# A PEER expert layer: four one-hot buffers, placing that begins with one group, and the list steps moved behind the first activation split

## Chip, cores and metric

One core of one Trainium2 chip runs the whole program. Its engines are named as in the profile: PE (matrix multiply; PEld is its weight load), DVE (vector), ACT (activation), POOL (GpSimd, which also issues the indirect transfers), SP (issues the plain transfers). The metric is the device time of one execution in microseconds; lower is better. The time before is the median of three runs, 1680.32 us (1677.39 to 1680.75).

## What is computed

A two-layer encoder trunk on x of 256 tokens by 1024 features, fp32. Layer 0 mixes tokens by multi-head latent attention, layer 1 by sparse attention. After each comes the part that matters here, a PEER mixer: every token picks 16 of 16,384 experts in each of 8 heads (128 picks per token), and the output is the weighted sum of the picked experts' rows:

```python
def per_block(args):                    # x_blk: 128 tokens, e_blk/g_blk: their picks and gates
    u = w_down[e_blk]
    a = jnp.einsum('td,ted->te', x_blk, u).astype(jnp.float32)
    hg = (jax.nn.gelu(a, approximate=False) * g_blk).astype(w_up.dtype)
    return jnp.einsum('te,ted->td', hg, w_up[e_blk]).astype(x_blk.dtype)
```

Each sublayer ends in x <- LayerNorm(alpha * x + sublayer(x)).

## The kernel before

**Numbers.** Every fp32 operand is split into two fp16 parts, `hi` (a cast on ACT, L166) and `lo` (the rest, on DVE, L175); a product is three matmuls (hi by hi, hi by lo, lo by hi). DVE also sums the remainders, which a check at the end uses.

**Weights.** The 128 x 1024 weight blocks come as one stream (`Stream`): `raw` (6 buffers) from HBM, then `hi` and `lo` (6 buffers each). `ws.get()` hands out a block, splits three blocks ahead and loads five more ahead of that. SP issues the loads of blocks at fixed places (L220); POOL issues those of listed blocks by indirect transfers with addresses from the table `up_at` (L218).

**PEER, down stage (d).** The kernel does not gather picks token by token. It multiplies all tokens with all 128 blocks of `down` (128 experts each), in 64 steps of two blocks (loop at L1511, `b0` = 0, 2, ..., 126). One step is 48 matmuls of 128 x 256. Meanwhile DVE chooses the experts (`choose`). Once they are chosen, the gates are **placed** into the matrix A (experts by tokens), four tokens to a group, 64 groups: `prepare` (L1357) builds a one-hot `hot` (L1361) and `gate` (L1363 on DVE, L1367 on ACT) for a group in buffers with the tags V and U, and `place` (L1370) multiplies them into G, 12 matmuls with those for `seen`, which counts the experts in use. A group is prepared in one step and placed behind the matmuls of the next. With `END = 8` the groups are spread so that the last is placed at `b0 = 120`. Where gates are placed already, a step's gelu is multiplied in by DVE (L1525).

**Lists.** When all groups are placed, `lists` (L1390) finds with DVE which experts any token uses. It is a generator with 23 stops: the loop takes three steps of it per `b0` (`list_on(3)`), the up stage one per block until block 11 (`HEAD - 9`), and then all that is left. Its results are the tables `up_at` and `act_at`. Rows of A go to DRAM by `store` (L1493, SP).

**Up stage (y).** The first `DENSE = 46` blocks of `up` are multiplied whole; of the others only listed rows, 72 blocks of 128 rows each. The first `HEAD = 20` dense blocks come in front, the other 26 stand among the listed ones (`_up_order`, L77). A dense block or one listed for both halves of the tokens is 12 matmuls of 128 x 512, one listed for one half is 6. For listed rows, `gather` (L1580) fetches the activations from DRAM by POOL into tiles with the tags V and U, three groups ahead. `cut(n)` (L1596) splits a pair of activations: `xh` on ACT, `xl` on DVE, four pairs deep. `cut(0)` stands at the start of the up stage. Stores go on until block 17, the first three groups are gathered at block 16. The stage ends in `finish` with the layer norm.

**Order.** A scheduler orders the instructions of each engine, except where the program writes the order out: what goes through `dve(...)` is kept in program order on DVE from the moment `chains["dve"]` is set (all groups placed) until the lists are done, and so is `pe(...)` on PE. In that stretch a list step, the lo split of a block, a product (L1525) and the lo half of a cut stand on DVE exactly as written. [...]

**Buffers.** The pool `ohp` has two buffers per tag, V and U, 2 KB per partition each. The one-hots, the lists' scratch and the gathered activations all use them, one after the other.

Of the kernel before, what the change touches and what calls it, by code (L numbers as in the profile page):

```python
# [15 lines left out]
AF = mybir.ActivationFunctionType  # L16
ALU = mybir.AluOpType
AX = mybir.AxisListType

P = 128  # L20
T = 256
D = 1024
NC = D // P
# [42 lines left out]
LEAST, MOST, ROW, SMALL = 64.0, 2.0 ** 40, 4.0, 2.0 ** -24  # L66
BOTH, MOSTLY = 128, 704
CHECKS = 7 * P
DENSE, HEAD = 46, 20
JB, JO, TB, ROWTAIL = 24, 16, 16, 32  # L70
BOTHS = JB + TB
LISTED = BOTHS + 2 * JO
END = 8
CHUNKED = 4


# [251 lines left out]
def tile_trunk(ctx: ExitStack, tc: tile.TileContext, ins, out: bass.AP, short, shared):  # L328
# [3 lines left out]
    def pool(name, bufs, **kw):  # L332
        return ctx.enter_context(tc.tile_pool(name=name, bufs=bufs, **kw))
# [5 lines left out]
    const = pool("const", 1)  # L339
    dram = pool("dram", 1, space=bass.MemoryType.DRAM)  # L340
    small = pool("small", 3)
    ohp = pool("ohp", 2)
    psp = pool("psp", 4, space=bass.MemoryType.PSUM)
    pyp, arena, mhalf, sound = shared["pyp"], shared["arena"], shared["mhalf"], shared["sound"]

# [3 lines left out]
    def ps(name):  # L349
        return psp.tile([P, 512], F32, tag="ps", name=name)  # L350
# [94 lines left out]
    def dve(emit):  # L445
        return link("dve", emit)
# [16 lines left out]
    def proj(o, blk, w=P, late=False):  # L463

        h, l = blk
        if late:
            for c in range(NC):
                mm(o, h[:, c * w : (c + 1) * w], xh[:, c, :], c == 0, False)
                mm(o, h[:, c * w : (c + 1) * w], xl[:, c, :], False, False)
            for c in range(NC):  # L470
                ins = mm(o, l[:, c * w : (c + 1) * w], xh[:, c, :], False, c == NC - 1)
            return ins
        for c in range(NC):
            s = slice(c * w, (c + 1) * w)
            ins = mm3(o, (h[:, s], l[:, s]), (xh[:, c, :], xl[:, c, :]), c == 0, c == NC - 1)
        return ins
# [690 lines left out]
    def peer(li):  # L1167
# [337 lines left out]
        def list_on(n):  # L1505
            for _ in range(n):
                next(listing[0], None)

        groups = prepared = 0
        ready = False  # L1510
        for b0 in range(0, NKEYS, 2):  # L1511
            p = ps(f"d{b0}")
            pv = p.rearrange("p (j t) -> p j t", t=T)
            chosen = ready
            for j in range(2):
                proj(pv[:, j, :], ws.get())
                ready = ready or spend(PACE)
            if b0 == 0:
                chains["pe"] = None
            t0 = 4 * groups  # L1520
            if t0 < T:
                nc.scalar.activation(A[:, b0 : b0 + 2, t0:], pv[:, :, t0:], AF.Gelu, scale=1.0 / unit)
            if t0 > 0:
                nc.scalar.activation(pv[:, :, :t0], pv[:, :, :t0], AF.Gelu, scale=1.0 / unit)
                dve(lambda: nc.vector.tensor_tensor(A[:, b0 : b0 + 2, :t0], A[:, b0 : b0 + 2, :t0], pv[:, :, :t0],  # L1525
                                                    op=ALU.mult))
            while groups < prepared:
                place(groups, b0 + 2)
                groups += 1
            if chosen:  # L1530
                left = max(1, (NKEYS - (END if short else 4) - b0) // 2)
                want = min(64 - groups, -(-(64 - groups) // left))
                assert want <= 3, b0
                for _ in range(want):
                    prepare(prepared, nc.gpsimd if want == 1 else nc.vector)
                    prepared += 1
            if short:
                if groups >= 32:
                    store(0, b0)
                    store(0, b0)  # L1540
                if groups == 64:
                    if listing[0] is None:
                        chains["dve"] = None
                        listing[0] = lists()
                    list_on(3)
                    store(1, b0)
                    store(1, b0)
        assert groups == 64, groups
        if not short:
            chains.pop("pe")  # L1550

        lnar = Arena(arena)
        y4 = [[py(2 * t + n, f"y{t}{n}") for n in range(2)] for t in range(2)]
        parts = {}

        def operand(k):
            if k % 2 == 0 and k not in parts:
                a = A[:, k : k + 2, :]
                slot = slice(k % NC, k % NC + 2)
                hh, al = xh[:, slot, :], xl[:, slot, :]  # L1560
                total = split.total("most")
                split.high(hh, a, A_UNIT)
                split.low(al, a, A_UNIT, hh, total)
                for j in range(2):
                    parts[k + j] = (hh[:, j, :], al[:, j, :])
            return parts[k]

        held = []

        def middle_loads():  # L1570
            held.append(load_x(lnar, keep))
            held.append(load_affine(lnar, li, 1))
            if last and short:
                least()
                split.seen = BOTH + split.n["most"]
                weigh_up(0, 0, split.seen)

        gathered, made = {}, {}

        def gather(g):  # L1580
# [15 lines left out]
        def cut(n):  # L1596
# [11 lines left out]
            dve(lambda: split.low(al, a, A_UNIT, hh, total))  # L1608
            made[n] = [(hh[:, j, :], al[:, j, :]) for j in range(2)]

        if short:
            cut(0)
            for i, (n, slot, tiles) in enumerate(USES):
                if i == FIRSTS[n]:
                    cut(n + 1)
                    if PAIRS[n][0] == "listed":
                        gather(PAIRS[n][1] + 3)
                if i < len(USES) - STAGGER:
                    rows(y4, made[n][slot], ws.get(), i == 0, False, tiles)
                if i < HEAD - 9:  # L1620
                    list_on(1)
                if i == HEAD - 9:
                    list_on(99)
                    chains.pop("dve")
                    chains.pop("pe")
                if i < HEAD - 3:
                    store(0, NKEYS)
                    store(1, NKEYS)
                if i == HEAD - 4:
                    assert stored == [NKEYS, NKEYS], stored  # L1630
                    for g in range(3):
                        gather(g)
                if i == len(USES) // 2:
                    middle_loads()
            items = [(made[n][slot], tiles) for n, slot, tiles in USES[-STAGGER:]]
        else:
            for k in range(NKEYS - STAGGER):
                rows(y4, operand(k), ws.get(), k == 0, False)
                if k == 64:
                    middle_loads()  # L1640
            items = [(operand(k), (0, 1)) for k in range(NKEYS - STAGGER, NKEYS)]
# [18 lines left out]
    def first(o):  # L1660

        queue = queue_of()
        idle = ps("idle")
        some = iotac.rearrange("p c k -> p (c k)")

        def busy(n, w=P):
            for _ in range(n):
                queue("pe", lambda: nc.tensor.matmul(idle[:, :w], iota16, some[:, :w], start=True, stop=True))

        def x_high(c, engine="act"):  # L1670
            queue(engine, lambda: split.high(xh[:, piece[c], :], xt[:, piece[c], :], X_UNIT, engine))

        def x_low(c):
            total = split.total("both")
            return queue("dve", lambda: split.low(xl[:, piece[c], :], xt[:, piece[c], :], X_UNIT, xh[:, piece[c], :],
                                                  total))

        def w_low(i):
            s = slice(512 * i, 512 * i + 512)
            total = split.total("both")  # L1680
            queue("dve", lambda: split.low(lo0[:, s], raw0[:, s], W_UNIT, hi0[:, s], total))

        def passes(w, x, *pieces):
            for c in pieces:
                for k in (2 * c, 2 * c + 1):
                    queue("pe", lambda: mm(o, w[:, k * P : (k + 1) * P], x[:, k, :], k == 0 and w is hi0 and x is xh,
                                           k == NC - 1 and x is xl))

        for i in range(2):
            s = slice(512 * i, 512 * i + 512)  # L1690
            queue("act", lambda: split.high(hi0[:, s], raw0[:, s], W_UNIT))
        w_low(0)
        w_low(1)
        for c in range(4):
            x_high(c)
            last = x_low(c)
        busy(WARM, 512)
        for c in range(2):
            passes(hi0, xh, c)
            passes(lo0, xh, c)  # L1700
        passes(hi0, xl, 0, 1)
        busy(2)
        for c in range(2, 4):
            passes(hi0, xh, c)
            passes(lo0, xh, c)
        passes(hi0, xl, 2, 3)
        return last
# [98 lines left out]
```

## Time and profile before

| what | us |
|---|---|
| median of the runs | 1680.32 |
| profiled execution | 1676.38 |
| its span | 1674.6 |
| PE busy in it | 1606.8 |
| layer 0: d stage, placing, up stage begin near | 142, 304, 533 |
| layer 1: d stage, placing, up stage begin near | 988, 1148, 1377 |
| listed rows of layers 0 and 1 begin on POOL near | 573, 1418 |

The profile comes from one execution. A row of a timeline has the start in us, the length in us, the engine, the line of the program, the operation, "out<-in" by the names of tiles, and a count; in brackets stands the idle time before it and what ended that. A row of waits reads "engine tile line <- what it waited for: us in total, times, longest". The windows give each engine's busy time in a stretch and PE's granted clock as a share of full speed.

### The profile page before, as it was taken

The numbers are of one execution on the slowest core, as the hardware profiler recorded it, in microseconds if no ns is written. First come the engines' busy times: TensorE is split into PE (matmuls) and PEld (weight loads), VectorE is DVE, ScalarE is ACT, GpSimd is POOL, SyncE is SP. The second block draws the span as 40 slices with busy tenths as digits, with TensorE's granted clock in tenths as the row PEclk, the third lists the DMA queues.
The fourth block names the chain that finished last, engine by engine and source line by source line (L and its number), as shares of the span: only waits on it lengthen the run. The fifth ranks groups of instructions, "written<-read, shape, count | busy, mean of one in ns | idle before, by whom it ended". The sixth has DMA issues, their size and how long they took to land.

```text
span 1674.6 us, 33334 instructions
## 1 busy us (share of the span) xinstructions
PE 1606.8 (96%) x12449; PEld 1164.4 (70%) x12449; DVE 1349.2 (81%) x3212; ACT 1064.7 (64%) x1863; POOL 527.6 (32%) x419
## 2 busy tenths in 40 slices
PE   9999999899998999999999999998999989999995
PEld 7678888799996444444577688887999974444442
DVE  8689999788998757676788799998889988566665
ACT  7666647688885446555578666565888764445553
POOL 2011255000000278877032012441000000788772
PEclk9999999999999999999999999999999999999998
DMA  9445656545757878888855555555447568678783
GB/s 348 158 166 174 199 180 210 172 162 172 240 176 235 284 232 279 268 279 269 287 192 180 169 192 181 188 196 194 152 157 246 184 205 292 228 260 267 258 281 121
DMA packets 139964, 361.44 MB, mean 216 GB/s; under 512 B 13713, under 2 KB 56849, under 8 KB 139793
## 3 DMA queue, kind: packets, MB, share of 16 engines
q1 hardware_dynamic: 112880, 268.51, 47.8%
q0 software_dynamic: 26624, 90.20, 16.5%
q8 instruction: 99, 1.62, 0.4%
q14 instruction: 73, 0.59, 0.1%
q10 hardware_dynamic: 288, 0.52, 0.1%
HBM read 333.35 MB, written 25.82 MB: 214 GB/s over the span
## 4 chain that ended last, share of the span: by engine, by line
PE 51%; issue 13%; DVE 11%; DMA 11%; POOL 10%; ACT 3%; SPq 0%; POOLq 0%; DVEq 0%; ACTq 0%
PE d L452 34%; DMA raw<-in_up,up_at 6%; PE y L452 5%; POOL raw L218 5%; DVE lo L175 5%; PE G L452 3%; PE pq L452 2%; PE seen L452 2%; ACT hi L166 2%; POOL V L1593 1%; POOL U L1587 1%; POOL V L1587 1%; DMA U<-abuf,act_at 1%; POOL U L1593 1%; PE qw L452 1%
## 5 line engine op out<-in xcount | busy, mean ns | idle before, releaser
L175 DVE SCALAR_TENSOR_TENSOR lo<-raw,hi 128x1024 f16<-128x1024 f32 (+2 forms) x550 | 696.8, 1277 | 207.5 <-ACT hi L166 203.4
L166 ACT ACTIVATE hi<-raw 128x1024 f16<-128x1024 f32 (+2 forms) x550 | 570.0, 1049 | 374.9 <-DMA raw<-in_up,up_at 166.9
L452 PE MATMUL d<-xh,lo 128*128 128x256 f16 x2048 | 559.3, 273 | 1.6 <-DVE lo L175 1.6
L452 PE MATMUL d<-xh,hi 128*128 128x256 f16 x2048 | 559.5, 273 | 0.0
L452 PE MATMUL d<-xl,hi 128*128 128x256 f16 x2048 | 559.3, 273 | 0.0
L452 PEld LDWEIGHTS <-hi 128*128 128x128 f16 x5016 | 489.3, 98 | 59.0 <-issue 1.5
L218 POOL DMA_INDIRECT raw<-in_up,up_at x144 | 182.5, 1268 | 612.1 <-DMA raw<-in_up 561.8
L452 PEld LDWEIGHTS <-xh 128*128 128x128 f16 x1904 | 185.4, 98 | 232.0 <-issue 12.9
L452 PE MATMUL y<-hi,xl 128*128 128x512 f16 x880 | 265.4, 381 | 11.1 <-DVE xl L175 11.1
L452 PE MATMUL y<-hi,xh 128*128 128x512 f16 x880 | 265.6, 381 | 5.2 <-ACT hi L166 2.8
L452 PE MATMUL y<-lo,xh 128*128 128x512 f16 x880 | 265.8, 381 | 3.6 <-DVE lo L175 3.6
L452 PEld LDWEIGHTS <-lo 128*128 128x128 f16 x2508 | 245.9, 98 | 33.1 <-DVE lo L175 3.6
L1367 ACT ACTIVATE gate<-hot,rest 128x128 f16<-128x128 f16 x512 | 167.3, 406 | 22.3 <-DVE hot L1361 20.7
L452 PEld LDWEIGHTS <-xl 128*128 128x128 f16 x952 | 93.0, 98 | 125.2 <-DVE xl L175 13.8
L255 POOL TENSOR_TENSOR lo<-raw,hi 128x1024 f16<-128x1024 f32 x27 | 62.0, 2295 | 213.6 <-ACT hi L253 182.1
L452 PE MATMUL G<-gate,hot 128*128 128x128 f16 x1024 | 98.2, 221 | 15.7 <-DVE gate L1363 15.7
L1361 DVE TENSOR_TENSOR hot<-iota,place 128x1024 f16<-128x1024 f16 x128 | 87.9, 688 | 26.5 <-PE G L452 25.7
L452 PEld LDWEIGHTS <-hot 128*128 128x128 f16 x1536 | 93.8, 114 | 17.6 <-DVE gate L1363 7.0
L452 PE MATMUL seen<-gate,hot 128*128 128x128 f16 x512 | 90.3, 220 | 0.0
L1282 POOL TENSOR_TENSOR arena<-arena 128x800 f32<-128x800 f16 x32 | 70.4, 2200 | 63.0 <-DVE arena L1279 63.0
L251 ACT ACTIVATE raw<-raw 128x1024 f32<-128x1024 f32 x27 | 28.5, 1056 | 93.1 <-DMA raw<-in_down 82.1
L1363 DVE TENSOR_TENSOR gate<-hot,gate 128x512 f16<-128x512 f16 x128 | 87.3, 682 | 0.0
(269 smaller groups left out, 1807.2 us busy)
## 6 DMA issues: line engine op xcount, KB each, us to landing
raw<-in_down SPq DMA_DIRECT2D x256, 512.0 KB, 3.4
raw<-in_up SPq DMA_DIRECT2D x92, 512.0 KB, 6.1
abuf<-arena SPq DMA_DIRECT2D x80, 256.0 KB, 4.1
raw<-in_peer_q SPq DMA_DIRECT2D x24, 512.0 KB, 4.4
raw<-in_dsa_qk SPq DMA_DIRECT2D x16, 512.0 KB, 4.3
raw<-in_mla_w_o SPq DMA_DIRECT2D x8, 512.0 KB, 5.2
arena<-in_peer_q SPq DMA_DIRECT2D x8, 512.0 KB, 5.3
raw<-in_dsa_v SPq DMA_DIRECT2D x8, 512.0 KB, 5.9
```

What stands on the lines that cost most here:

```text
L166: return nc.scalar.copy(o, src) if unit == 1.0 else nc.scalar.mul(o, src, unit)
L175: return nc.vector.scalar_tensor_tensor(o, src, unit, hi, op0=ALU.mult, op1=ALU.subtract, accum_out=total)
L218: self.nc.gpsimd.indirect_dma_start(t, None, table, bass.IndirectOffsetOnAxis(ap=at, axis=0))
L251: self.act(lambda: nc.scalar.mul(raw, raw, unit))
L255: nc.gpsimd.tensor_tensor(lo, raw, hi if short else hi.bitcast(F32), op=ALU.subtract)
L452: return pe(lambda: nc.tensor.matmul(o, l, r, start=start, stop=stop, skip_group_check=True))
L1282: nc.gpsimd.tensor_tensor(o.rearrange("p k c -> p c k"), same, cell[t][:, h, :, None].to_broadcast([P, CELLS, TOPK]), op=ALU.mult)
L1361: nc.vector.tensor_tensor(hot, iota4[:, None].to_broadcast([P, 2, P, 4]), place16[:, :, None, four].to_broadcast([P, 2, P, 4]), op=ALU.is_ ...
L1363: engine.tensor_tensor(gate[:, 0], hot[:, 1].rearrange("p c j -> p j c"), gate16[:, four, None].to_broadcast([P, 4, P]), op=ALU.mult)
L1367: nc.scalar.mul(gate[:, 1, j, :], hot[:, 1, :, j], rest[:, t : t + 1])
L1587: nc.gpsimd.indirect_dma_start(t[:, 2 * slot : 2 * slot + 2, :].rearrange("p a b -> p (a b)"), None, abuf, bass.IndirectOffsetOnAxis(ap=at ...
L1593: nc.gpsimd.indirect_dma_start(t[:, 2 + h, :], None, halves, bass.IndirectOffsetOnAxis(ap=at, axis=0))
```

## The change

Six edits. [...] `END` goes from 8 to 6, and a step may prepare at most one group more than are placed already, so that the steps place 1, 2, 3 and then two groups each, the last at `b0 = 122`. `cut(0)` moves from the start of the up stage into the last d step, behind its matmuls and ahead of its products. The last d step takes no list steps any more. `HEAD` goes from 20 to 24: block 15 is where the lists must be done, 20 where the first gathers are issued, and 22 dense blocks stay among the listed ones. In the first projection of layer 0, `busy` issues four small filler matmuls rather than two, with another tile as the moving operand. The functions `gather` and `cut` are moved up unchanged so that the loop can call them.

```diff
-DENSE, HEAD = 46, 20
+DENSE, HEAD = 46, 24
-END = 8
+END = 6
...
-    ohp = pool("ohp", 2)
+    ohp = pool("ohp", 4 if short else 2)
...
             if b0 == 0:
                 chains["pe"] = None
+            if short and b0 == NKEYS - 2:
+                cut(0)
             t0 = 4 * groups
...
-                for _ in range(want):
+                for _ in range(min(want, 1 + groups)):
                     prepare(prepared, nc.gpsimd if want == 1 else nc.vector)
                     prepared += 1
...
-                    list_on(3)
+                    if b0 < NKEYS - 2:
+                        list_on(3)
...
         if short:
-            cut(0)
             for i, (n, slot, tiles) in enumerate(USES):
...
         def busy(n, w=P):
+            moving = some[:, :w] if w > P else iota4[:, :, 0]
             for _ in range(n):
-                queue("pe", lambda: nc.tensor.matmul(idle[:, :w], iota16, some[:, :w], start=True, stop=True))
+                queue("pe", lambda: nc.tensor.matmul(idle[:, :w], iota16, moving, start=True, stop=True))
...
-        busy(2)
+        busy(4)
...
-    nc = bacc.Bacc("TRN2", target_bir_lowering=False, num_devices=1)
+    nc = bacc.Bacc("TRN2", target_bir_lowering=False, num_devices=1, dynamic_dma_scratch_size=8192)
```

More of the change, by code (lines that the diff above doesn't have):

```diff
@@ L1507, in list_on @@
                 next(listing[0], None)
[L1509 to L1533, printed above, removed]
-                for _ in range(want):
[L1535 to L1544, printed above, removed]
-                    list_on(3)
-                    store(1, b0)
-                    store(1, b0)
@@ L1548, in peer @@
[L1548 to L1576, printed above, removed]
         gathered, made = {}, {}
@@ L1609, in cut @@
             made[n] = [(hh[:, j, :], al[:, j, :]) for j in range(2)]
+        groups = prepared = 0
+        ready = False
+        for b0 in range(0, NKEYS, 2):
+            p = ps(f"d{b0}")
+            pv = p.rearrange("p (j t) -> p j t", t=T)
+            chosen = ready
+            for j in range(2):
+                proj(pv[:, j, :], ws.get())
+                ready = ready or spend(PACE)
+            if b0 == 0:
+                chains["pe"] = None
+            if short and b0 == NKEYS - 2:
+                cut(0)
+            t0 = 4 * groups
+            if t0 < T:
+                nc.scalar.activation(A[:, b0 : b0 + 2, t0:], pv[:, :, t0:], AF.Gelu, scale=1.0 / unit)
+            if t0 > 0:
+                nc.scalar.activation(pv[:, :, :t0], pv[:, :, :t0], AF.Gelu, scale=1.0 / unit)
+                dve(lambda: nc.vector.tensor_tensor(A[:, b0 : b0 + 2, :t0], A[:, b0 : b0 + 2, :t0], pv[:, :, :t0],
+                                                    op=ALU.mult))
+            while groups < prepared:
+                place(groups, b0 + 2)
+                groups += 1
+            if chosen:
+                left = max(1, (NKEYS - (END if short else 4) - b0) // 2)
+                want = min(64 - groups, -(-(64 - groups) // left))
+                assert want <= 3, b0
+                for _ in range(min(want, 1 + groups)):
+                    prepare(prepared, nc.gpsimd if want == 1 else nc.vector)
+                    prepared += 1
+            if short:
+                if groups >= 32:
+                    store(0, b0)
+                    store(0, b0)
+                if groups == 64:
+                    if listing[0] is None:
+                        chains["dve"] = None
+                        listing[0] = lists()
+                    if b0 < NKEYS - 2:
+                        list_on(3)
+                    store(1, b0)
+                    store(1, b0)
@@ new lines, in peer, with operand @@
+        assert groups == 64, groups
+        if not short:
+            chains.pop("pe")
+        lnar = Arena(arena)
+        y4 = [[py(2 * t + n, f"y{t}{n}") for n in range(2)] for t in range(2)]
+        parts = {}
+        def operand(k):
+            if k % 2 == 0 and k not in parts:
+                a = A[:, k : k + 2, :]
+                slot = slice(k % NC, k % NC + 2)
+                hh, al = xh[:, slot, :], xl[:, slot, :]
+                total = split.total("most")
+                split.high(hh, a, A_UNIT)
+                split.low(al, a, A_UNIT, hh, total)
+                for j in range(2):
+                    parts[k + j] = (hh[:, j, :], al[:, j, :])
+            return parts[k]
@@ L1611, in peer, with middle_loads @@
+        held = []
+        def middle_loads():
+            held.append(load_x(lnar, keep))
+            held.append(load_affine(lnar, li, 1))
+            if last and short:
+                least()
+                split.seen = BOTH + split.n["most"]
+                weigh_up(0, 0, split.seen)
         if short:
-            cut(0)
             for i, (n, slot, tiles) in enumerate(USES):
```

## Prediction

> **What bounds the kernel now.** I read the page's engine table first, then TensorE's (PE's) waits over the whole span, then the stages one by one.
>
> ```profile
> PE 1606.8 (96%) x12449; PEld 1164.4 (70%) x12449; DVE 1349.2 (81%) x3212; ACT 1064.7 (64%) x1863; POOL 527.6 (32%) x419
> PE 51%; issue 13%; DVE 11%; DMA 11%; POOL 10%; ACT 3%; SPq 0%; POOLq 0%; DVEq 0%; ACTq 0%
> PE G L452 <- DVE gate L1363: 15.7, 8, 4.0
> PE y L452 <- DVE xl L175: 11.1, 2, 5.7
> PE y L452 <- ACT xh L166: 2.4, 2, 1.3
> ```
>
> PE is busy 96% of the span, so an edit gains only if it removes PE idle time. The rows of waits give total us, times and the longest. Two waits stand out, and each belongs to one place in each layer: the first one-hots of placing (G behind the DVE gate, 15.7 us in eight waits), and the first activations of the up stage (y behind xl, 11.1 us in two, with 2.4 us behind xh just before). The chain is the second message: 10% of it is POOL and 11% DMA, so some stage is held by transfers that POOL issues even while PE looks full. A view of the stages by window shows which.
>
> ```profile
> 304.00:326.00 22.00, 14.43 (x143) 12.21 (x142) 16.39 (x32) 15.77 (x41) 0.00 (x0) 0.84 0.49 155
> 326.00:532.00 206.00, 206.00 (x2229) 188.86 (x2226) 183.00 (x341) 161.65 (x410) 0.00 (x0) 1.00 0.57 184
> 573.00:795.00 222.00, 220.55 (x1022) 99.79 (x1020) 141.34 (x279) 120.19 (x139) 174.44 (x144) 1.00 0.79 262
> ```
>
> Columns after the length: PE, PEld, DVE, ACT, POOL, granted clock, DMA share, GB/s. When placing begins (304 to 326) PE works 14.43 of 22 us at a mean clock of 0.84; the steady part after it (326 to 532) has no idle time at all. From 573 to 795, the listed rows, PE is full too (220.55 of 222), but POOL issues 144 transfers there.
>
> **Part 1: placing begins with one group, from four buffers.** In the trace the first two steps place three groups each.
>
> ```profile
> 306.08 0.25 PE L452 MATMUL G<-gate,hot 128*128 128x128 f16 x1 [0.26 <-DVE gate L1363]
> 307.83 0.22 PE L452 MATMUL G<-gate,hot 128*128 128x128 f16 x1 [0.88 <-DVE gate L1363]
> 312.62 0.26 PE L452 MATMUL G<-gate,hot 128*128 128x128 f16 x1 [3.96 <-DVE gate L1363]
> 324.73 0.25 PE L452 MATMUL G<-gate,hot 128*128 128x128 f16 x1 [2.46 <-DVE gate L1363]
> 304.13 1.29 DVE L1361 TENSOR_TENSOR hot<-iota,place 128x1024 f16<-128x1024 f16 x2
> 309.53 0.69 DVE L1361 TENSOR_TENSOR hot<-iota,place 128x1024 f16<-128x1024 f16 x1
> 311.88 0.68 DVE L1363 TENSOR_TENSOR gate<-hot,gate 128x512 f16<-128x512 f16 x1
> 371.65 5.24 PE d L452 x48
> 378.23 5.24 PE d L452 x48
> ```
>
> Two one-hots are made back to back at 304.13. The third starts at 309.53, because it needs the buffer of the first and that buffer is free only after group 0's matmuls. PE waits 0.26 + 0.88 + 3.96 + 2.46 = 7.56 us in layer 0; 15.7 - 7.56 = 8.1 us are left for layer 1. By the new rule (left = 32 at the first step, where 31 gave three) the steps place 1, 2, 3, then two groups each to the end: still 64 groups, so PE's work is unchanged. Four buffers hold the three groups of the third step. Each group costs DVE 0.69 + 0.68 us, so two groups take 2.7 us beside 5.24 us of d matmuls: covered. The last two rows, from the chain in order of time, are a step with two groups, 6.58 us, so a group takes PE 0.67 us. The three-group step needs 3 x 1.4 us plus two lo splits of 1.2 and the placings, some 7.5 us on DVE, against 7.25 us on PE; I leave 0.5 us of wait per layer for it.
>
> The stall also slows the clock, as single microseconds show.
>
> ```profile
> 311.00:312.00 1.00, 0.00 (x0) 0.50 0.82 291
> 316.00:317.00 1.00, 1.00 (x6) 0.50 0.00 0
> 317.00:318.00 1.00, 1.00 (x10) 0.87 0.00 0
> 1160.00:1162.00 2.00, 2.00 (x18) 0.91 0.03 8
> ```
>
> After the restart at 312.62 the clock is 0.50 until about 317.2, which loses half of 4.6 us, 2.3 us; in layer 1 (restart at 1157.6, full speed near 1161.8) 2.1 us. [...] Sum of part 1: 15.7 - 1.0 + 4.4 = **19 us**.
>
> **Part 2: first activations split ahead of list steps.** At the hand-over from d to y:
>
> ```profile
> 531.86 0.27 PE L452 MATMUL d<-xh,lo 128*128 128x256 f16 x1
> 533.21 0.60 PE L452 MATMUL y<-hi,xh 128*128 128x512 f16 x2 [1.07 <-ACT xh L166]
> 539.90 0.61 PE L452 MATMUL y<-hi,xl 128*128 128x512 f16 x1 [5.66 <-DVE xl L175]
> 531.08 0.69 DVE L1525 TENSOR_TENSOR arena<-arena,d 128x512 f32<-128x512 f32 x1 [3.05 <-ACT d L1524]
> 535.87 0.68 DVE L1525 TENSOR_TENSOR arena<-arena,d 128x512 f32<-128x512 f32 x1
> 539.15 0.68 DVE L175 SCALAR_TENSOR_TENSOR xl<-arena,xh 128x512 f16<-128x512 f32 x1
> 542.00:543.00 1.00, 1.00 (x5) 0.73 1.14 346
> 1388.00:1390.00 2.00, 2.00 (x8) 0.74 1.05 403
> ```
>
> The last two rows are windows of PE alone (length, busy, clock, DMA). DVE is on one written-out order here: product of the last step but one (531.08), list steps, two lo splits, product of the last step (535.87), list steps, and only then xl at 539.15. In the changed order xl stands before the last product and no list step follows that product inside the loop. The d matmuls end near 532.0 (first row). If the product at 531.08 no longer waits its 3.05 us, it starts near 528; the list steps behind it took until 533.6 minus the same 3 us, 530.5; then two lo splits (the 2.3 us before 535.87) and xl, 0.7 us: xl is done near 533.5 and PE needs it near 532.9. PE would gain 5.66 + 1.07 - 0.6 = 6.1 us and the slow clock after it (half speed from 539.9 to about 542.3, 1.2 us; in layer 1, by the last row, until about 1389, 2.5 us). That is **7.3 and 8.6 us at the start of y**, if nothing later takes it back.
>
> **Part 3: list steps later, dense front 24 rather than 20.** This takes it back, I think. END 6 puts the last placing, and so the start of the lists, one step of 5.3 us later. Six list steps remain in the loop rather than twelve; the rest stand one per dense block, and the tables that tell POOL what to fetch are complete at block 15 rather than 11. POOL waits for them:
>
> ```profile
> 572.20 0.20 DVE L1483 TENSOR_SCALAR up_at<-U 128x72 int32<-128x72 f32 x1
> 573.33 1.24 POOL L218 DMA_INDIRECT raw<-in_up,up_at  x1 [280.87 <-DMA raw<-in_up]
> 793.19 1.25 POOL L218 DMA_INDIRECT raw<-in_up,up_at  x1 [0.30 <-issue]
> POOL raw L218 <- DVE lo L175: 4.3, 4, 2.4
> 569.45 0.35 PE L1467 MATMUL moved<-sent,to 128*128 128x32 f16 x8
> 564.23 2.60 PE y L452 x12
> L218 POOL DMA_INDIRECT raw<-in_up,up_at x144: 933/1238/1996, 573.3 to 1643.9; - x144
> 577.35 0.95 POOL L1587 DMA_INDIRECT V<-abuf,act_at  x1 [0.30 <-issue]
> DMA to landing us min/median/max: 3.2/5.8/9.9
> ```
>
> POOL starts at 573.33, 1.1 us after up_at, and issues 144 transfers to 794.44 with 0.30 us between them; only 4.3 us are waits for a free raw buffer. That is 221 us for 144, 1.54 us each: in this stage POOL never rests, and its start sets its end. The new start: the table needs the last `moved` matmuls, which PE runs behind block 15. From 532.9, sixteen blocks of 2.60 us end at 574.5; POOL followed those matmuls by 573.33 - 569.45 = 3.9 us, so it starts near 578 at PE's pace. DVE's own pace says the same: from xl at 539.15 to up_at it took 33 us, and the new order adds four lo splits (4.6), two xl (1.4) and six list steps (an estimate of 0.7 each, as long as a hot: 4.2), so up_at comes 43 us after 533.5, near 577. I take 4 to 5 us later than now, measured from the end of d (578 against 573.33). POOL gets back the waits for buffers (about 3 us net, because PE presses harder) and a little from four fewer dense splits: its end is unchanged within some 2 us. Is PE really tied to it? In the listed stage of layer 1 PE already waits eight times:
>
> ```profile
> PE y L452 <- DVE lo L175: 2.9, 5, 0.7
> PE y L452 <- ACT hi L166: 2.0, 3, 0.8
> ```
>
> and the four dense blocks moved to the front (4 x 2.59 = 10.4 us) are cover that this stage loses. So of the 15.9 us of part 2, I keep **2 us**, 1 per layer. Bounds: all of it (15.9), or a loss of 4 per layer if the start is 8 us later.
>
> **Part 4: what should cost nothing.** The two extra `busy` matmuls are no longer than the G row at 306.08, 0.25 us each. Stores start one step later but have four more blocks to finish in. More gather buffers (eight tiles rather than four) let POOL run further ahead; the number of issues stays 144. The halved descriptor area shows in no row. A transfer lands 5.8 us after its issue (median) and issues are 1.54 us apart, so about four are under way. [...] I take nothing, with both ends open: 0, or some of the 1.1 us by which issues differ already (0.93 to 2.00).
>
> **Sum.** 19 + 2 = 21 us. The profiled execution has a span of 1674.6 and a time of 1676.38 us, 3.9 us under the median of the runs, 1680.32; 1676.4 - 21 = 1655.4 there, and on the scale of the median **1659.3 us**.
>
> **Rivals.**
> - *The up stage keeps its gain*: POOL's issues get shorter, or the lists end earlier. For it: PE's waits in layer 0's listed stage are under 2 us, and the issues vary from 0.93 to 2.00 us. Against: the full POOL rows. 19 + 15.9 = 35 us, 1645.
> - *Gathers crowd ahead of the raw rows.* With eight tiles, POOL's order can put four more groups (about ten issues, 15 us) in front of raw rows that PE needs first. The 10.4 us of longer front cover part; 4 to 10 us per layer are lost: about 1668.
> - *The change does not do what it says in placing*: if DVE's work rather than the buffers makes the third one-hot late, stalls of about 5 us per layer stay. About 1670.
> - *Slower: the halved descriptor area throttles POOL.* Place: the 288 issues of both listed stages, which run back to back. From 21/288 = 0.073 us more per issue the gain is gone; at 0.25 us more it is 72 us, 1659 + 72 = 1731. Against: four transfers under way now, and issues that start at 0.95 us when they come close upon each other (577.35).
>
> **Chances.** Forecast (1654 to 1665) 0.53; up stage keeps its gain 0.20; gathers crowd 0.13; placing half done 0.08; throttled 0.06. The range 1644 to 1670 leaves out the throttled case, half of the crowding, and parts of the third and of the low end, about 0.2. 0.2% is 3.4 us, about what a measurement of this kernel can tell from no change: faster 0.88, same 0.04, slower 0.08.
>
> **What would show it.** Right: G's waits on gate under 2 us in all, and no window at clock 0.50 near the start of placing; y's wait on xl under 1 us each; the first indirect issue 44 to 47 us after the last d matmul (41.4 now), then 144 issues without a pause, and new PE waits for lo or hi in the listed stage, 5 us or more per layer. Wrong: a first issue no later than now with PE full to the end (then 1645), a mean issue longer than now (then slower), or a long PE wait at the first listed rows (crowding).

## The result, and the profile after

The change made the kernel slower: 1703.15 us median (1699.58 to 1705.04) beside 1679.64 for the kernel before, ratio 1.0139, 95% interval 1.0118 to 1.0161, some 23 us. The forecast was 1659.3.

The page of the changed kernel (engines, then the chain), its waits of PE over the whole span, and then two rows of waits of the kernel before:

```profile
PE 1622.3 (95%) x12451; PEld 1166.2 (68%) x12451; DVE 1348.2 (79%) x3212; ACT 1064.9 (63%) x1865; POOL 522.8 (31%) x419
PE 57%; DVE 11%; issue 10%; DMA 9%; POOL 9%; ACT 3%; SPq 2%; DVEq 0%; POOLq 0%; ACTq 0%
PE y L452 <- ACT hi L166: 30.0, 16, 6.6
PE y L452 <- DVE lo L175: 9.5, 20, 0.7
PE y L452 <- ACT xh L166: 8.3, 2, 4.2
PE G L452 <- DVE gate L1363: 3.6, 2, 2.1
PE y L452 <- DVE xl L175: 1.9, 2, 0.9
```

```profile
PE y L452 <- DVE lo L175: 3.6, 6, 0.7
PE y L452 <- ACT hi L166: 2.8, 4, 0.8
```

Both waits that the change was aimed at are nearly gone: G behind gate 15.7 to 3.6 us, y behind xl 11.1 to 1.9. Others have grown: behind hi, lo and xh y waited 8.8 us in all (2.8, 3.6 and 2.4), and now waits 47.8. PE also took 15.5 us longer over its matmuls (1622.3 us busy rather than 1606.8, with two matmuls more): its clock was lower in places. So the up stage is where to look. Windows of the changed kernel (length, then PE, PEld, DVE, ACT, POOL, clock, DMA share, GB/s):

```profile
304.00:326.00 22.00, 21.29 (x242) 19.68 (x243) 21.00 (x40) 21.49 (x55) 0.00 (x0) 1.00 0.55 172
520.00:546.00 26.00, 24.19 (x115) 10.96 (x113) 19.61 (x55) 10.61 (x15) 0.00 (x0) 1.00 1.06 345
546.00:575.00 29.00, 28.35 (x161) 13.32 (x161) 28.62 (x69) 15.17 (x17) 0.37 (x1) 1.00 0.66 244
600.00:650.00 50.00, 39.51 (x164) 16.56 (x162) 20.09 (x40) 16.98 (x20) 39.03 (x37) 0.90 0.61 202
```

Where placing begins, PE worked 14.43 of 22 us at clock 0.84; now it works 21.29 at full clock. From 600 to 650, among the first listed rows, it worked 48.55 of 50 and now works 39.51, at clock 0.90. The rows that mark the stages of layer 0 in the changed kernel, and then the last y matmul of before:

```profile
520.43 0.27 PE L452 MATMUL d<-xh,lo 128*128 128x256 f16 x1
567.77 0.35 PE L1467 MATMUL moved<-sent,to 128*128 128x32 f16 x8
573.49 0.20 DVE L1483 TENSOR_SCALAR up_at<-U 128x72 int32<-128x72 f32 x1
574.63 1.55 POOL L218 DMA_INDIRECT raw<-in_up,up_at  x1 [284.75 <-DVE act_at L1488]
823.86 0.38 PE L452 MATMUL y<-hi,xl 128*128 128x512 f16 x1
```

```profile
806.89 0.38 PE L452 MATMUL y<-hi,xl 128*128 128x512 f16 x1
```

d ends at 520.7, 11.4 us earlier than before (532.1). But the table `up_at` is ready at 573.7, 1.3 us *later* than before (572.4), and the last y matmul ends at 824.2, 17.0 us later than before (807.3). So two distances have grown: from the end of d to `up_at`, 40.3 to 53.0 us; and from `up_at` to the end of y, 234.9 to 250.5. Layer 1 shows the same: 41.5 to 53.6, and 239.7 to 252.0. These two distances, read in the same way from every trace, are the columns of the table below.

What fills the second one shows in POOL's issues of raw rows alone, in windows of before and then of the changed kernel (POOL's busy time with the count of issues, PE's clock, DMA):

```profile
573.00:600.00 27.00, 6.86 (x6) 1.00 0.63 198
600.00:625.00 25.00, 9.62 (x9) 1.00 0.75 250
625.00:650.00 25.00, 8.93 (x8) 1.00 0.83 283
```

```profile
573.00:600.00 27.00, 6.57 (x6) 0.87 0.62 203
600.00:625.00 25.00, 6.10 (x6) 0.93 0.64 212
625.00:650.00 25.00, 5.02 (x5) 0.86 0.58 193
```

In these three windows POOL as a whole is about as busy as before (58.9 us of 77, before 60.5) and issues 17 raw rows rather than 23. In the changed kernel's timeline the others are gathers of activations, for later groups:

```profile
594.08 1.27 POOL L218 DMA_INDIRECT raw<-in_up,up_at  x1 [0.30 <-issue]
595.65 0.94 POOL L1518 DMA_INDIRECT V<-abuf,act_at  x1 [0.30 <-issue]
...
602.37 1.99 POOL L1518 DMA_INDIRECT V<-abuf,act_at  x1 [0.30 <-issue]
604.66 1.24 POOL L218 DMA_INDIRECT raw<-in_up,up_at  x1 [0.30 <-issue]
...
641.62 1.87 PE L452 MATMUL y<-hi,xh 128*128 128x512 f16 x4 [6.28 <-ACT hi L166]
```

Ten microseconds lie between two raw rows here, six gathers stand between them, and PE later waits 6.28 us for the hi of a raw row.

### The profile page after: what moved, and what is told of

Read it like the earlier page. It is cut to its first block, busy times and chain, and to the rows that moved or that the text cites. A ratio compares the mean times of both kernels' runs of the same rounds, so it can differ in the third digit from the quotient of the medians.

```text
span 1702.6 us, 33172 instructions
## 1 busy us (share of the span) xinstructions
PE 1622.3 (95%) x12451; PEld 1166.2 (68%) x12451; DVE 1348.2 (79%) x3212; ACT 1064.9 (63%) x1865; POOL 522.8 (31%) x419
## 3 DMA queue, kind: packets, MB, share of 16 engines
q1 hardware_dynamic: 112880, 268.51, 46.6%
## 4 chain that ended last, share of the span: by engine, by line
PE 57%; DVE 11%; issue 10%; DMA 9%; POOL 9%; ACT 3%; SPq 2%; DVEq 0%; POOLq 0%; ACTq 0%
PE d L452 33%; PE y L452 12%; DVE lo L175 5%; POOL raw L218 4%; PE G L452 3%; DMA raw<-in_up,up_at 3%; DMA V<-abuf,act_at 2%; PE pq L452 2%; PE seen L452 2%; SPq L1500 2%; POOL U L1518 1%; ACT hi L166 1%; POOL V L1518 1%; POOL U L1524 1%; POOL V L1524 1%
## 5 line engine op out<-in xcount | busy, mean ns | idle before, releaser
L452 PE MATMUL y<-lo,xh 128*128 128x512 f16 x880 | 270.5, 386 | 10.0 <-DVE lo L175 9.5
L452 PE MATMUL y<-hi,xl 128*128 128x512 f16 x880 | 269.7, 386 | 1.9 <-DVE xl L175 1.9
```

Of the source, the lines that this page charges most:

```text
L452: return pe(lambda: nc.tensor.matmul(o, l, r, start=start, stop=stop, skip_group_check=True))
```

## The experiments

Two theories: **crowding** (with eight gather tiles the order on POOL puts gathers ahead of rows that PE needs first) and **late start** (the lists end later after d, and POOL with them). A third, **area**, was the prediction's rival on the slower side. The kernels ran in five groups on chips that aren't equally fast (before took 1676.67 to 1697.1 us), so each ratio is to the kernel before in its own group. The columns are layer 0 / layer 1, in us of the profiled run.

| run | ratio (95% interval) | d end to `up_at` | `up_at` to y end |
|---|---|---|---|
| before (first profile) | 1 | 40.3 / 41.5 | 234.9 / 239.7 |
| the change (result) | 1.0139 (1.0118 to 1.0161) | 53.0 / 53.6 | 250.5 / 252.0 |
| group 1: area | 0.9989 (0.9965 to 1.0014) | 41.5 / 41.9 | 249.0 / 246.2 |
| buffers | 1.0061 (1.0039 to 1.0084) | 42.3 / 40.7 | 260.3 / 267.1 |
| onegroup | 1.0001 (0.9978 to 1.0024) | 41.7 / 41.7 | 246.9 / 245.0 |
| limit | 0.9995 (0.9966 to 1.0024) | 53.0 / 52.5 | 241.4 / 238.0 |
| group 2: changed | 1.0158 (1.0108 to 1.0207) | 52.8 / 53.5 | 248.7 / 249.9 |
| onelim | 0.9899 (0.9854 to 0.9944) | 40.5 / 40.9 | 235.0 / 235.4 |
| all8 | 0.9919 (0.9891 to 0.9947) | 46.8 / 45.4 | 236.8 / 237.2 |
| limit20 | 0.9954 (0.9929 to 0.9978) | 48.0 / 47.9 | 236.2 / 240.6 |
| group 3: crowd | 1.0075 (1.0046 to 1.0104) | 41.4 / 41.0 | 257.8 / 269.6 |
| early3 | 0.9893 (0.9843 to 0.9943) | 42.8 / 43.5 | 244.7 / 240.0 |
| head24 | 0.9867 (0.9821 to 0.9913) | 40.1 / 39.3 | 247.3 / 245.4 |
| end6 | 0.9938 (0.9916 to 0.9960) | 47.5 / 46.6 | 245.7 / 243.3 |
| group 4: order | 0.9859 (0.9834 to 0.9883) | 41.6 / 42.4 | 233.1 / 233.3 |
| best | 0.9784 (0.9760 to 0.9808) | 36.8 / 36.3 | 237.0 / 234.8 |
| limit8 | 0.9925 (0.9895 to 0.9954) | 45.6 / 43.7 | 237.8 / 238.8 |
| limit_b | 1.0031 (1.0005 to 1.0056) | 53.1 / 52.7 | 238.0 / 239.0 |
| group 5: late24 | 0.9835 (0.9812 to 0.9857) | 40.2 / 39.2 | 236.1 / 235.3 |
| early24 | 0.9805 (0.9778 to 0.9831) | 36.0 / 35.9 | 237.1 / 236.9 |

On the chips of groups 1 and 3 the second column is some 10 us longer for most kernels that gather into four tiles; in group 1 that holds even for area, which is the kernel before but for the descriptor area. In the profiles of these two groups y also has waits that stand behind "issue", for which the profile shows no cause (15.2 us in area, 7.2 to 37.3 us in the others); in those of the other groups it has none. The second column is compared within a group only.

### The area alone

```diff
-num_devices=1)
+num_devices=1, dynamic_dma_scratch_size=8192)
```

> The kernel before with the descriptor area halved to 8192 and nothing else. Theory 'crowding' (eight gather tiles let POOL's order put gathers ahead of raw rows that TensorE needs first) and theory 'late start' (the lists now end later against the end of d, so POOL starts no earlier): the area costs nothing, 1680 us, mean of a raw issue near 1.24 us. Theory 'area' (fewer transfers can be under way): slower, up to the 23 us of the whole change, 1690 to 1703.

0.9989: nothing. The grouped row of area's raw issues:

```profile
L218 POOL DMA_INDIRECT raw<-in_up,up_at x144 | 176.8, 1228 | 634.7 <-DMA raw<-in_up 284.3 <-DVE act_at L1488 281.6 <-issue 35.8
```

An issue takes 1.228 us on average; the same row of the kernel before has 1.268. Issues did not get longer. The theory of the area falls. The prediction, which took nothing for this edit, was right in that. That 8192 is half of the area, as the prediction has it, was not shown: the kernel before does not set the size.

### Buffers alone, placing alone

`buffers` is area with

```diff
-    ohp = pool("ohp", 2)
+    ohp = pool("ohp", 4 if short else 2)
```

> The kernel before with the halved area and four one-hot buffers; placing, list steps, HEAD 20 and END 8 as before. POOL's order becomes crowded (9 + 3 gathers before the fourth raw row). Theory 'crowding': POOL starts near 571 us as before, but TensorE waits 5 to 15 us more per layer for hi in the first third of the listed rows: 1685 to 1700. Theory 'late start': nothing is later, and the buffers shorten the first placing waits a little: 1672 to 1681.

`onegroup` is the kernel before, with two buffers and

```diff
-                for _ in range(want):
+                for _ in range(min(want, 1 + groups)):
```

> The kernel before with placing begun by one group (1, 2, then three), two buffers, everything else as before. Both theories: the waits of G behind gate fall from 15.7 to 5 to 9 us, d ends 5 to 8 us earlier per layer, and the lists and POOL's first issue move earlier with it, so all of it is kept: 1664 to 1672. If the listed stage isn't tied to POOL's start: the same. If something else sets the end: 1680.

buffers: slower, as crowding said, though its placing improved and d ended at 522.0 (area: 532.0). From `up_at` on it took 11.3 and 21.0 us longer than area on the same chip. onegroup: no gain, against both theories. The wait of G in buffers, then in onegroup:

```profile
PE G L452 <- DVE gate L1363: 5.4, 4, 2.1
PE G L452 <- DVE gate L1363: 15.9, 7, 2.6
```

Four buffers alone take 10 of the 15.7 us of before; the one-group start alone takes nothing. With two buffers no single wait is as long as before (2.6 us rather than 4.0), but the sum stays, so beginning with one group is worth nothing without the buffers.

### Gathers kept to four tiles

`limit` is the changed kernel with

```diff
-            t = oh_tile("VU"[g % 2])
+            if g == 0:
+                kept.extend(oh_tile("VU"[i % 2]) for i in range(4))
+            t = kept[g % 4]
```

> The changed kernel with its gathers kept to four tiles; the one-hots keep their four buffers, all else as changed. POOL's order is mixed evenly again. Theory 'crowding': POOL still starts near 574.6, and the stage takes as long from there as before (233.6 and 238.8 us to the end of y, where the changed kernel took 249.5 and 251): 28 us less, 1675, TensorE's waits for hi 15 us or less. Theory 'late start' alone: the waits stay, 1695 to 1703.

`changed` is the changed kernel itself beside others, and `onelim` is the kernel before with the area, four buffers, the one-group start and the four gather tiles, so that lists, `HEAD`, `END` and the first split stay as before.

> The changed kernel as it is, to stand on the same chip as the others of this group. If the chip doesn't matter to the comparison: ratio 1.012 to 1.016 as in the result, the stage from POOL's first issue to the end of y near 250 us in both layers.

> The kernel before with the halved area, four one-hot buffers, placing begun by one group, and gathers kept to four tiles; the list steps, HEAD 20, END 8 and the first split as before. Theory 'crowding': the order on POOL is that of before, d ends some 10 us earlier in each layer and POOL starts 8 to 10 us earlier with it; POOL's stage lasts as before, so the gain of placing is kept: 16 to 20 us, ratio 0.988 to 0.991. Rival 'POOL's start doesn't set the end' (late landings of the rows do): 0.997 to 1.003.

limit lost the slowdown and gained nothing: its stage from `up_at` on is shorter (241.4 / 238.0, where area on the same chip takes 249.0 / 246.2), its lists still late. Its ratio is 0.9995, where crowding alone had expected 1675 us of 1680 and late start alone 1695 or more. onelim gained what the prediction gave to placing: 0.9899 of 1680 is 17 us. G's wait there, with the four buffers, and the wait on xl, which it keeps:

```profile
PE G L452 <- DVE gate L1363: 3.6, 2, 2.1
PE y L452 <- DVE xl L175: 10.9, 2, 5.7
```

### Is it the order or the tiles?

`crowd` is onelim without the four-tile rule (so eight tiles). `order` is crowd with every transfer that POOL issues queued in program order:

```diff
+    def behind(self, emit):
+        if self.line is None:
+            self.line = emit().ins
+            return
+        with self.tc.issue_after(self.line):
+            self.line = emit().ins
...
-                    self.nc.gpsimd.indirect_dma_start(t, None, table, bass.IndirectOffsetOnAxis(ap=at, axis=0))
+                    self.behind(lambda: self.nc.gpsimd.indirect_dma_start(t, None, table,
+                                                                          bass.IndirectOffsetOnAxis(ap=at, axis=0)))
```

and the gathers go through `behind` too. Where it can be compared, two runs of one kernel keep one order: the 92 rows of DVE from 539.79 to 599.23 in best (below) stand in the same order in early24, the same kernel on another chip.

> As onelim (0.990), but gathers may use all eight tiles: crowding alone, with the gain of placing kept. Theory 'crowding': POOL starts near 562 us as in onelim, TensorE then waits for hi in the first third of the listed rows, and from the end of d to the end of y it takes 288 to 300 us rather than 276: 24 to 48 us over both layers, ratio 1.004 to 1.018. If crowding needs the longer front to hurt: 0.988 to 0.993.

> As crowd (1.0075: halved area, eight gather tiles, placing begun by one group), but every transfer that POOL issues is queued in the order of the program, raw rows and gathers evenly mixed; all eight tiles stay in use. If it is the order that costs: the waits of y go and the ratio is that of onelim, 0.986 to 0.993. If eight tiles cost by more transfers under way or by the memory they use: it stays near 1.0075, above 1.000.

crowd 1.0075, order 0.9859, with the same tiles and the same area. They ran on different chips, but head24 and early3, with four tiles on the chip of crowd, stand at 0.9867 and 0.9893, so that chip alone does not make 1.0075. Until 608 POOL has issued 8 raw rows in crowd, 15 in order, and 12 in onelim with its four tiles. The first gap between raw rows in crowd, with twelve gathers in it, then in order, with seven:

```profile
568.16 0.93 POOL L218 DMA_INDIRECT raw<-in_up,up_at  x1 [0.30 <-ACT hi L166]
...
585.43 0.94 POOL L218 DMA_INDIRECT raw<-in_up,up_at  x1 [0.30 <-issue]
```

```profile
567.18 0.94 POOL L226 DMA_INDIRECT raw<-in_up,up_at  x1 [0.30 <-issue]
...
577.32 0.94 POOL L226 DMA_INDIRECT raw<-in_up,up_at  x1 [0.30 <-DMA V<-abuf,act_at]
```

The window from 600 to 650 in crowd, then in order:

```profile
600.00:650.00 50.00, 43.59 (x175) 17.73 (x175) 23.48 (x45) 20.84 (x25) 33.28 (x30) 0.83 0.64 203
```

```profile
600.00:650.00 50.00, 50.00 (x234) 22.64 (x232) 33.31 (x63) 28.51 (x33) 38.35 (x32) 1.00 0.81 265
```

POOL issues about as many transfers (30 and 32), but PE does 175 matmuls in the one and 234 in the other. So it is the order, as far as two chips can be compared: eight tiles cost nothing where it is held. In crowd the waits of y stand behind "issue" (30.5 us in 40 waits), though hi had been expected, so the single waits are not traced to a late row there; in the changed kernel they are (30.0 us behind hi).

### The lists, and the front

Single edits on onelim: `head24` has `HEAD = 24`, `end6` has `END = 6`, and `early3` has `cut(0)` ahead of the last products with the list steps kept:

```diff
+            if short and b0 == NKEYS - 2:
+                cut(0)
             t0 = 4 * groups
```

> As onelim (0.990) with HEAD 24: four dense blocks are moved from between the listed rows to the front. Theory 'late start': what POOL reads raw rows into comes free four blocks later, so the first raw row is issued 5 to 10 us later against the end of d, and the stage ends later by about as much: ratio 0.996 to 1.002. If the longer front pays for itself with cover: 0.987 to 0.992.

> As onelim (0.990) with END 6: the lists begin one step of 5.3 us later. If POOL's start sets the end: 2 to 5 us per layer, 0.992 to 0.996. If not: 0.988 to 0.991.

> As onelim (0.990), but the first activations are split ahead of the last product, with the three list steps behind that product kept where they are. y's wait on xl (10.9 us in all) falls under 4. If TensorE's own work sets the end of the stage: 4 us less per layer, 0.984 to 0.987. If POOL's start sets it (1.4 us later by two xl splits): 0.989 to 0.992, and TensorE's waits come back in the listed rows.

And from the other side, with gathers on four tiles: `all8` is the changed kernel with `HEAD = 20`, `END = 8`; `limit20` with `HEAD = 20`; `limit8` with `END = 8`; `limit_b` is limit once more. `best` is early3 with `HEAD = 24`.

> The changed kernel with gathers kept to four tiles, HEAD 20 and END 8; the first activations stay split ahead of list steps. If the stage is tied to POOL's start: like onelim within 0.3% (y starts 7 us earlier, but POOL doesn't), ratio 0.987 to 0.992. If TensorE's own work sets the end: 7 us less per layer than onelim, 0.980 to 0.984.

> The changed kernel with gathers kept to four tiles and HEAD 20 (END 6 as changed). Theory 'late start': POOL's first issue, 54 us behind the end of d with HEAD 24, comes 45 to 49 us behind it with HEAD 20, and the end moves with it: ratio 0.992 to 0.996, between limit (0.9995) and all8. If the start doesn't matter: as limit, 0.997 to 1.002.

> The changed kernel with gathers kept to four tiles and END 8 (HEAD 24 and the early split as changed). If the parts add up (onelim 0.990, HEAD 24 -0.3%, early split without its list steps +0.2%): 0.986 to 0.992. If HEAD 24 costs with lists that end this late: 0.994 to 1.000.

> The kernel limit once more, beside limit8, on whatever chip this group gets: END 6 against END 8 with HEAD 24. If its 0.9995 holds: 0.996 to 1.002, and END 6 costs 0.5 to 1% with HEAD 24. If the parts add up: 0.990 to 0.995.

> onelim with both edits that were no worse than it: HEAD 24 and the first activations split ahead of the last product (list steps kept). If their gains (0.3% and 0.1%, each within its interval) add: 0.981 to 0.986. If POOL's rate binds: 0.986 to 0.991.

head24 went against the late start as it was put: the longer front by itself costs nothing (0.9867). What costs is the list steps that leave the d loop. early3 shows no gain of the split over head24 in its group (0.9893), and end6 alone loses (0.9938; its first column is 7.0 us longer than that of onelim in layer 0). best, limit8 and limit_b form a row in one group: best keeps twelve list steps in the loop, limit8 drops the last step's three, and limit_b with `END = 6` drops three more. `up_at` and the last y matmul of layer 0 in best, limit8 and limit_b:

```profile
559.52 0.20 DVE L1483 TENSOR_SCALAR up_at<-U 128x72 int32<-128x72 f32 x1
796.31 0.38 PE L452 MATMUL y<-hi,xl 128*128 128x512 f16 x1
```

```profile
569.99 0.20 DVE L1483 TENSOR_SCALAR up_at<-U 128x72 int32<-128x72 f32 x1
807.58 0.38 PE L452 MATMUL y<-hi,xl 128*128 128x512 f16 x1
```

```profile
573.14 0.20 DVE L1483 TENSOR_SCALAR up_at<-U 128x72 int32<-128x72 f32 x1
810.93 0.38 PE L452 MATMUL y<-hi,xl 128*128 128x512 f16 x1
```

`up_at` comes 10.5 and then 3.2 us later, and the end of y 11.3 and then 3.4 us later. In layer 1, measured from the end of layer 0's y, the first pair differs by 11.7 us in `up_at` and 15.7 in the end, the second by 8.7 and 8.9. The end follows `up_at` about one for one in three of the four, and by 4.0 us more in the other. In the first column, three dropped steps add 8.8 and 7.4 us (36.8 to 45.6, 36.3 to 43.7), three more add 7.5 and 9.0: about one dense block of 2.60 us for each step, since a step outside the loop has a block to itself. In ratio: 0.9784, 0.9925, 1.0031, or 1.4% and 1.1%. With `HEAD = 20` the remaining steps are taken together at block 11, and the first column grows less with the early split: 42.8, 46.8 and 48.0 in early3, all8 and limit20 for the same two edits, 5.2 us in layer 0 rather than 16.3. So `HEAD = 24` made them dearer in this distance (groups 2 and 3 stand for `HEAD = 20`, group 4 for 24).

The waits of y tell the two causes apart. Those on hi and xh in limit_b, which has four tiles and the late lists, and the one on xh in limit20:

```profile
PE y L452 <- ACT hi L166: 10.6, 7, 2.3
PE y L452 <- ACT xh L166: 8.5, 2, 4.3
PE y L452 <- ACT xh L166: 16.7, 2, 8.9
```

The changed kernel waits 8.3 us on xh too, so that wait comes with the late lists and not with the tiles: it stands at the first gathered activations (4.21 us at 590.70). With the shorter front of limit20 it is twice as long, so the four blocks of `HEAD = 24` did cover part of the late start. The wait on hi is what eight tiles add: 30.0 us in the changed kernel, 10.6 here.

### What the early split is worth

`late24` is head24 and `early24` is best, once more and side by side; they differ in the place of `cut(0)` alone.

> head24 once more, beside best (next), on one chip: the two differ only in where the first activations are split. As before: 0.984 to 0.991, y's wait on xl about 11 us in all.

> best once more, beside late24. If the early split is worth what the prediction's part 2 said (15.9 us, when the list steps stay where they are): 0.9% under late24. If it is worth only the wait that is seen to go (11.1 to 4.8 us): 0.4% under it. If best owed its lead to its chip: the same as late24.

0.9835 and 0.9805: 0.3%, some 5 us (3.0 us between the medians, 1651.26 and 1648.24). The intervals overlap, so this is not clear of noise; it is of the size of the wait that goes. The wait of y on xl in late24, then in early24:

```profile
PE y L452 <- DVE xl L175: 10.6, 2, 5.8
```

```profile
PE y L452 <- DVE xl L175: 4.4, 2, 2.5
```

best (and early24, the same kernel) beats both kernels: 1643.66 us beside 1680.37 in its group, and 1648.24 beside 1676.67. Its PE is busy 98% of a span of 1643.0 us.

## Why the prediction was wrong, point by point

- **Part 1 (placing, 19 us): right.** G's wait fell to 3.6 us (the sum allowed 1.0, the sign was under 2) and the slow clock at 311 to 317 is gone: it is 1.00 in the whole window from 304 to 326. Alone with a good order on POOL it gave 17 us (onelim). That the buffers, not DVE's work, made the third one-hot late is shown by buffers (5.4 us) beside onegroup (15.9).
- **Part 2 (first split, 15.9 us): right at the start of y.** The waits on xl and xh there fell from 13.5 us to 1.9, 11.6 us where 12.2 was forecast, and the clock from 520 to 546 is 1.00 (0.87 in the kernel before). But three list steps were dropped for it, and they cost more (next point). With the list steps kept, the split takes 6.2 us of wait on xl away and gives 3 to 5 us, not clear of noise (early24 against late24).
- **Part 3 (lists later): the step that failed first.** "I take 4 to 5 us later than now, measured from the end of d" was 12.7 us: POOL's first issue came 53.9 us after the end of d, where before it came 41.2 and the sum had 46. The sum took sixteen blocks at PE's 2.60 us and 3.9 us of lag, 45 us from the start of y at 520.5. The last of the `moved` matmuls, though, started at 567.77 rather than near 562, and POOL followed 6.9 us behind. DVE was behind PE:

```profile
525.24 0.69 DVE L1560 TENSOR_TENSOR arena<-arena,d 128x512 f32<-128x512 f32 x1 [2.79 <-ACT d L1559]
PE base L1433 <- DVE n L1427: 3.6, 2, 2.1
571.78 0.17 DVE L1478 COPY keys<-moved 128x16 f32<-128x16 f32 x1
```

  The product of the last d step waited 2.79 us for its gelu, where before, at 535.87, it had not waited, and the next list step is written behind it; DVE worked only 19.61 of 26 us from 520 to 546. PE then waited for a list step (base behind n), which it does not in the kernel before. From 546 to 575 DVE was busy 28.62 of 29 us, and the copy of `moved` stood without a pause behind other work of DVE, 4.0 us after the last of these matmuls began. The sum by DVE's own pace priced the six list steps at 0.7 us each. That is what they take when they stand together, three from 531.69 to 533.59 in the kernel before; dealt out one to a block they cost about 2.7 each, 16.3 us per layer (best to limit_b). The stated bound ("a loss of 4 per layer if the start is 8 us later") had the right direction and was not taken.
- **"Its end is unchanged within some 2 us": wrong.** This assumed that POOL's 144 issues come in an order that PE can use. They took 230.7 rather than 221.1 us in layer 0, and 232.3 rather than 226.5 in layer 1, and PE was the one to wait.
- **Rival "gathers crowd ahead of the raw rows": what happened, and under-priced.** It stood at 4 to 10 us per layer and 0.13. Four tiles against eight in the changed kernel is 1.0031 against 1.0158, 1.3% or 21 us, 10 to 11 us per layer in the second column. The 10.4 us of longer front did not cover it. It also should have been added to a later start, not weighed as its alternative. Its sign, "a long PE wait at the first listed rows", came (4.21 us at 590.70), but from the late lists, as limit_b shows.
- **Rival "area": refuted** (area). **Rival "placing half done": refuted** (onelim). **Rival "up stage keeps its gain", 1645:** best landed there (1643.66; 1648.24 as early24), with the list steps in the loop and gathers on four tiles. That the figures agree is luck: of its 36.7 us (28.4 as early24) some 17 are placing and 3 to 5 the split, and the rest, which stands with `HEAD = 24`, was in no sum.
- **Longer front:** counted as a loss of cover in the listed rows; head24 shows no loss, and limit20 shows that the front covers part of a late start.

Counted in ratios from best to the changed kernel: three list steps out of the loop cost 0.0141, `END = 6` another 0.0106, eight gather tiles 0.0127. The first two are measured in one group. The last compares two groups on different chips; the traces show it too (second column 238.0 against 248.7, 239.0 against 249.9, and the wait on hi 10.6 against 29.3).

Open: what makes the second column some 10 us longer on the chips of groups 1 and 3, where y's waits stand behind "issue", and what `HEAD = 24` gains by itself (0.9867 against 0.9899 for onelim, on different chips).

## What to carry to other kernels

More buffers change more than the wait that they remove: where a scheduler fills a queue with whatever is ready, a freed buffer is a licence to go ahead (1.0075 in crowd and 0.9859 in order, with the same eight tiles, on two chips), so look at the order of the queue that those buffers feed and write it out if something urgent shares it. When work is taken out of a loop and dealt out one step to a block, its price is a block for each step, not its own duration (here some 2.7 us rather than 0.7), whenever a later engine waits for the last of it. A gain ahead of a stage is kept only if what starts that stage's bound engine moves with it (here d ended 11.4 us earlier, `up_at` came 1.3 us later, and y ended 17.0 us later).

## What the runs showed of the hardware that was not expected

The same kernel before took 1676.67 to 1697.1 us in the five groups. With `dynamic_dma_scratch_size=8192` and nothing else the time was the same (0.9989), and the mean issue was no longer (1.228 us; 1.268 in the kernel before).

In crowd, waits that were short one by one went with a low clock of PE. Two windows of PE alone in crowd (length, busy, clock, DMA share, GB/s), then two in late24:

```profile
616.00:617.00 1.00, 1.00 (x3) 0.50 0.00 0
617.00:618.00 1.00, 1.00 (x6) 0.96 0.41 111
```

```profile
535.00:536.00 1.00, 1.00 (x4) 0.50 0.92 315
536.00:537.00 1.00, 1.00 (x6) 1.00 1.00 367
```

There the clock was 0.50 in every microsecond from 600 to 617, while PE was held up until 612 by short waits (behind "issue" none of y's in the whole run took more than 1.8 us); it rose 5 us after the last of them. In late24 PE restarted at 530.39 after its 5.8 us of wait on xl, and the clock was full at 536, 5.6 us later. The prediction had read 4.6 and 4.2 us from the kernel before.
